# Expert feed-forward on one Trainium2 core: the gate's second pass moved behind its first, more work put in branches, a rare path moved to the start, an eighth weight buffer

## The chip, the cores and the metric

One Trainium2 chip, one of its cores. The time is device microseconds of one execution. Three runs of the kernel before took 1893.26, 1894.47 and 1895.01 us; the median is 1894.47. Fp32 weights lie in the chip's memory and are streamed once per execution.

## The reference, cut to what matters

256 tokens of width 1024 pass two layers (a pooling mixer with a dense feed-forward, then a delta-rule mixer with a mixture of experts) and a second block with three attentions and a feed-forward. The part around the change is the mixture of 8 experts, two for each token:

```python
def moe_ffn(h, router_w, router_b, w_gate, w_up, w_down):
    ...
    logits = (t @ router_w).astype(jnp.float32) + router_b.astype(jnp.float32)
    top_vals, top_idx = lax.top_k(logits, TOP_K)
    top_w = jax.nn.softmax(top_vals, axis=-1)
    gates = jnp.sum(jax.nn.one_hot(top_idx, N_EXPERTS, dtype=jnp.float32) * top_w[..., None], axis=1)
    for e in range(N_EXPERTS):
        y = swiglu(t, w_gate[e], w_up[e], w_down[e]).astype(jnp.float32)
        out = out + gates[:, e:e + 1] * y
```

Each expert has 1024 x 3584 gate and up weights and 3584 x 1024 down weights, 44 MB in all three. The kernel computes an expert only for the tokens that chose it, 64 on average.

## The kernel before, in words

**The weights.** `Stream.load` (L285 on) fetches one tile of the expert stream into the next buffer of the pool `rawm`, on SP's queue (L297). A tile holds 128 x 4096 floats (2 MB); the first two hold 128 x 2048. The pool has `RAWS_M` = 7 buffers. Tiles are loaded in the order of use (`plan_moe`): gate, up, then the down weights of the chunk before. A load goes out when its buffer's last readers are through.

**The experts.** `expert_loop` walks 8 experts x 4 chunks of the hidden width (1024, 1024, 1024, 512). A chunk of full width takes two tiles each of gate, up and down; the last chunk one each. `gather` (L1051) packs an expert's tokens into up to 128 columns by matmul. Per chunk, for the first 64 tokens ("main", L1108): gate, then SiLU on ACT (L1137), up, then the product `hid` on DVE (L1141), transposes (L1165), and the down matmuls (L1160) of the chunk before. For tokens 64 to 95 ("extra"): under `tc.If(count[e] > 64)` (L1142) both the gate's and the up's second passes stand together behind the up matmuls (L1114), into the PSUM tile `gx`; then `hidx` on ACT and DVE (L1146, L1147), its transposes (L1170) and their copy `hTx` (L1172), all in every chunk; and `extra_down` under a second `If` (L1175, matmuls L1122). The branches stand on PE only.

```python
with self.tc.If(count[e] > 64):
    extra(0, xg, wg, w // 4)
    extra(1, xg, wu, w // 4)
```

So gate, up and down tiles of a chunk are in use until the branch behind the up pass is through. The framework schedules the order on each engine itself and treats a branch's body as one unit; in the trace the branch stands ahead of the matmuls of the chunk's last up tile.

**The scatter.** When an expert's last down chunk is done, one chunk into the next expert, its rows are added to `h`: for each half of the tokens, matmuls with the first 64 rows (L1186), then with the second tokens' rows (L1189, always), then an add on DVE (L1193). The PSUM pool `most` has three buffers, called pt.

**The rare path.** `rare` (L1490 to L1498) covers experts with over 96 tokens. It issues loads ahead up to `RAWS_M - 2`, reads the largest count into a register of each engine (L1495) and branches twice (over 96, over 224; L1497). The body (`overflow`, L1500 on) holds all eight experts' work for 128 more tokens each, on PE, ACT, DVE and SP, with two weight buffers as its room. With these inputs it is never entered. It is called when expert 4 is done, one chunk into expert 5:

```python
if e0 == 4:
    self.rare(pg, pt, pd)
```

Of the kernel before, what the change touches and what calls it, by code (L numbers as in the profile page):

```python
# [9 lines left out]
F32 = mybir.dt.float32  # L10
# [10 lines left out]
KD = D // 128  # L21
# [4 lines left out]
FFC = (1024, 1024, 1024, 512)  # L26
RAW_D = 3072
RAW_M = 4096
RAWS_M = 7
FIRST_M = (2048, 2048)  # L30
SPARE_2 = list(range(2, 6)) + list(range(85, 91))
LN_EXP = "natural_log_exp_and_others"
# [291 lines left out]
class KB:  # L324
# [757 lines left out]
    def expert_loop(self, wk, pg, pt, pd):  # L1082

        nc, C, V = self.nc, self.C, self.nc.vector
        mm = nc.tensor.matmul
        st = self.stm
        self.pins[2] = 0
        lists, spreads = {0: self.gather(0, wk, pt)}, {}
        cnt = wk.tile([128, 1], F32, name="cntf", bufs=1)
        self.cnti = wk.tile([128, 1], I32, name="cnti", bufs=1)  # L1090
        counts = wk.tile([128, NE], I32, name="counts", bufs=1)
        V.tensor_copy(counts, self.pos[:, 2])
        V.tensor_reduce(cnt, self.pos[:, 2], axis=AX.X, op=OP.max)
        V.tensor_copy(self.cnti, cnt)
        gx = pg.tile([128, 2, 256], F32, name="gx")
        self.dx = pd.tile([128, 512], F32, name="dx")
        dx = self.dx[:, :256]
        for t in (gx, self.dx):
            V.memset(t, 0.0)
        chunks = [(e, c) for e in range(NE) for c in range(len(FFC))]  # L1100
        acc = {}
        count = {}
        prev = None

        def main(p, xg, ws, w):
            for k in range(KD):
                for s in range(2):
                    mm(p[s * 64:(s + 1) * 64, :w], xg[:, k, 0:64], ws[k][:, s * w:(s + 1) * w],  # L1108
                       start=k == 0, stop=k == KD - 1)

        def extra(r, xg, ws, w):
            for k in range(KD):
                for q in range(4):
                    mm(gx[q * 32:(q + 1) * 32, r, :w], xg[:, k, 64:96], ws[k][:, q * w:(q + 1) * w],  # L1114
                       start=k == 0, stop=k == KD - 1, skip_group_check=True)

        def extra_down(hTx, ws, c):
            n = len(ws) // 4
            for f, w in enumerate(ws):
                g, j = divmod(f, n)  # L1120
                for q in range(4):
                    mm(dx[q * 32:(q + 1) * 32], hTx[:, j, g * 32:(g + 1) * 32], w[:, q * 256:(q + 1) * 256],  # L1122
                       start=c == 0 and f == 0, stop=c == len(FFC) - 1 and f == len(ws) - 1, skip_group_check=True)

        for i in range(len(chunks) + 1):
            cur = None
            if i < len(chunks):
                e, c = chunks[i]
                w = FFC[c]
                if c == 0:  # L1130
                    count[e] = nc.values_load(counts[0:1, e:e + 1], engines=(mybir.EngineType.PE,), min_val=0, max_val=NT)
                xg = lists[e]
                wg = [st.plain("moe_w_gate") for _ in range(KD)]
                p = pg.tile([128, 512], F32, name="pg")
                main(p, xg, wg, w // 2)
                hid = wk.tile([128, 512], F32, name="hid")
                nc.scalar.activation(hid[:, :w // 2], p[:, :w // 2], AF.Silu)  # L1137
                wu = [st.plain("moe_w_up") for _ in range(KD)]
                p = pg.tile([128, 512], F32, name="pu")
                main(p, xg, wu, w // 2)  # L1140
                V.tensor_tensor(hid[:, :w // 2], p[:, :w // 2], hid[:, :w // 2], op=OP.mult)  # L1141
                with self.tc.If(count[e] > 64):  # L1142
                    extra(0, xg, wg, w // 4)
                    extra(1, xg, wu, w // 4)
                hidx = wk.tile([128, 256], F32, name="hidx")
                nc.scalar.activation(hidx[:, :w // 4], gx[:, 0, :w // 4], AF.Silu)  # L1146
                V.tensor_tensor(hidx[:, :w // 4], gx[:, 1, :w // 4], hidx[:, :w // 4], op=OP.mult)  # L1147
                if c == 1:
                    spreads[e] = self.spread(e, wk, pt)
                if c == 2 and e + 1 < NE:  # L1150
                    lists[e + 1] = self.gather(e + 1, wk, pt)
            if prev:
                e0, c0, hT, hTx = prev
                if c0 == 0:
                    acc[e0] = pd.tile([128, 512], F32, name="dacc")
                wd = [st.plain("moe_w_down") for _ in range(FFC[c0] // 128)]
                for f, wf in enumerate(wd):
                    s, j = divmod(f, len(wd) // 2)
                    for n in range(2):
                        mm(acc[e0][n * 64:(n + 1) * 64], hT[:, j, s * 64:(s + 1) * 64], wf[:, n * 512:(n + 1) * 512],  # L1160
                           start=c0 == 0 and f == 0, stop=c0 == len(FFC) - 1 and f == len(wd) - 1)
            if i < len(chunks):
                p = pt.tile([128, 4, 128], F32, name="pt")
                for j in range(w // 256):
                    nc.tensor.transpose(p[:, j], hid[:, j * 128:(j + 1) * 128], C["ident"])  # L1165
                cur_hT = wk.tile([128, 4, 128], F32, name="hT")
                nc.scalar.copy(cur_hT[:, :w // 256], p[:, :w // 256])  # L1167
                p = pt.tile([128, 2, 128], F32, name="pt")
                for j in range(w // 512):
                    nc.tensor.transpose(p[:, j], hidx[:, j * 128:(j + 1) * 128], C["ident"])  # L1170
                cur_hTx = wk.tile([128, 2, 128], F32, name="hTx")
                V.tensor_copy(cur_hTx[:, :w // 512], p[:, :w // 512])  # L1172
                cur = (e, c, cur_hT, cur_hTx)
            if prev:
                with self.tc.If(count[e0] > 64):  # L1175
                    extra_down(hTx, wd, c0)
            if prev and c0 == len(FFC) - 1:
                first, more = spreads.pop(e0)
                y = wk.tile([128, 512], F32, name="y", bufs=1)
                nc.scalar.copy(y, acc.pop(e0))  # L1180
                yx = wk.tile([128, 256], F32, name="yx", bufs=1)
                V.tensor_copy(yx, dx)
                for t in range(2):
                    ps = [pt.tile([128, 512], F32, name="pt") for _ in range(2)]
                    for n in range(2):
                        mm(ps[n], first[n * 64:(n + 1) * 64, t], y[n * 64:(n + 1) * 64], start=True, stop=True)  # L1186

                    for n in range(4):
                        mm(ps[n // 2][:, (n % 2) * 256:(n % 2 + 1) * 256], more[:, n, t], yx,  # L1189
                           start=False, stop=True, skip_group_check=True)  # L1190
                    for n in range(2):
                        hs = self.h[:, t, n * 512:(n + 1) * 512]
                        self.late = [V.tensor_tensor(hs, ps[n], hs, op=OP.add)]  # L1193
                if e0 == 4:
                    self.rare(pg, pt, pd)
            prev = cur

    def block2(self, st):
# [290 lines left out]

    def rare(self, pg, pt, pd):  # L1490

        t = self.stm.where[self.stm.i][0]
        while self.stm.next_load < min(t + RAWS_M - 2, len(self.stm.tiles)):
            self.stm.load()
        most = self.nc.values_load(self.cnti[0:1, 0:1], min_val=0, max_val=NT)  # L1495
        for first in (96, 224):
            with self.tc.If(most > first):  # L1497
                self.overflow(first, pg, pt, pd)  # L1498
# [81 lines left out]
def build(ctx, tc, I, out):  # L1580
# [6 lines left out]
    with kb.pool("mkv") as mkp:  # L1587
# [7 lines left out]
        with kb.pool("moe") as pl:  # L1595
# [4 lines left out]
            kb.wsps.close()  # L1600
            kb.stm.raw = raws.enter_context(kb.pool("rawm", RAWS_M, side="right"))
            kb.experts(raws)
# [24 lines left out]
```

## Time and profile before

| what | value |
|---|---|
| median of three runs | 1894.47 us |
| the profiled execution's own time | 1892.89 us |
| its span, first to last instruction | 1891.1 us |
| PE busy | 1758.4 us (93%) |
| DVE, ACT, POOL busy | 698.5, 594.6, 30.2 us |
| expert weights | 169 loads on SP's queue, 167 of 2048 KB |
| mean granted TensorE clock | 0.986 |

A busy share is a mean over stages: the expert stage lies between some 500 and 1413 us, and the rest of the span is the two dense parts around it. PE is TensorE's matmuls, PEld its weight loads, a q behind an engine's name its sequencer. In a timeline, a number in brackets behind a row is the engine's idle time before it and the arrow names what ended it.

### The profile page before, as it was taken

How to read it: one execution, taken by the hardware profiler on the slowest of the kernel's cores; microseconds unless marked ns; L12 is line 12 of the kernel's file. 1: busy time of each engine (PE TensorE's matmuls, PEld its weight loads, DVE VectorE, ACT ScalarE, POOL GpSimd, SP SyncE). 2: the span in 40 equal slices, each digit the busy share in tenths (PEclk: the TensorE clock that was granted, in tenths of full speed). 3: DMA queues.
4: the chain of work that ended last, by engine and by line, in shares of the span. 5: the costliest groups of instructions: out<-in, count | busy, mean ns of one | idle time of the engine just before them, and what ended most of it. 6: DMA issues, size and time to landing. Idle time of an engine off the chain costs nothing. (4 is left out here: it accounts for less than half of the span.)

```text
span 1891.1 us, 28195 instructions
## 1 busy us (share of the span) xinstructions
PE 1758.4 (93%) x12123; PEld 1201.5 (64%) x12123; DVE 698.5 (37%) x1365; ACT 594.6 (31%) x1043; POOL 30.2 (2%) x23
## 2 busy tenths in 40 slices
PE   7999999999887888889999889999987999999999
PEld 6898979998633333434434435344347778988987
DVE  6656578765400101000010100100016677665554
ACT  5544465445310101001010000100014657764443
POOL 0000000000000000000000000000002000002000
PEclk9999999999999999999999989999998999999999
DMA  8554543201499999999899989899943322445452
GB/s 328 198 192 179 179 169 122 101 35 56 189 425 425 426 425 426 425 425 384 360 377 425 379 361 383 338 425 426 374 199 134 134 101 101 179 156 201 179 189 79
DMA packets 40633, 501.55 MB, mean 265 GB/s; under 512 B 4497, under 2 KB 4881, under 8 KB 7441
## 3 DMA queue, kind: packets, MB, share of 16 engines
q1 hardware_dynamic: 40176, 498.59, 65.4%
q8 instruction: 129, 2.11, 0.5%
q10 hardware_dynamic: 288, 0.52, 0.1%
q14 instruction: 40, 0.32, 0.1%
HBM read 498.05 MB, written 1.05 MB: 264 GB/s over the span
## 5 line engine op out<-in xcount | busy, mean ns | idle before, releaser
L320 DVE TENSOR_TENSOR wlo<-raw,whi 128x1024 fp32r<-128x1024 f32 (+1 forms) x266 | 309.7, 1167 | 203.6 <-ACT whi L319 199.4
L319 ACT CAST whi<-raw 128x1024 fp32r<-128x1024 f32 (+1 forms) x276 | 274.0, 1000 | 262.9 <-PE pt L387 173.6
L386 PE MATMUL pt<-xTh,whi 128*128 128x256 f32 x1120 | 320.0, 286 | 3.8 <-ACT zT L786 1.5
L387 PE MATMUL pt<-xTl,whi 128*128 128x256 f32 x1120 | 318.6, 285 | 0.0
L388 PE MATMUL pt<-xTh,wlo 128*128 128x256 f32 x1120 | 318.0, 284 | 0.0
L1108 PE MATMUL pu<-raw,xg 128*64 128x512 f32 (+1 forms) x1024 | 208.6, 547 | 22.1 <-DMA raw<-in_w_moe_dram 16.3
L1108 PE MATMUL pg<-raw,xg 128*64 128x512 f32 (+1 forms) x1024 | 203.3, 546 | 21.1 <-DMA raw<-in_w_moe_dram 11.6
L386 PEld LDWEIGHTS pt<-xTh,whi 128*128 128x128 f32 x1120 | 212.5, 190 | 6.2 <-ACT zT L786 1.7
L387 PEld LDWEIGHTS pt<-xTl,whi 128*128 128x128 f32 x1120 | 212.3, 190 | 1.4 <-DVE xTl L393 0.3
L388 PEld LDWEIGHTS pt<-xTh,wlo 128*128 128x128 f32 x1120 | 211.8, 189 | 0.8 <-issue 0.5
L1160 PE MATMUL dacc<-raw,hT 128*64 128x512 f32 x896 | 204.4, 598 | 7.1 <-DMA raw<-in_w_moe_dram 4.7
L1147 DVE TENSOR_TENSOR hidx<-gx,hidx 128x256 f32<-128x256 f32 (+1 forms) x32 | 12.5, 391 | 494.0 <-ACT hidx L1146 494.0
L1108 PEld LDWEIGHTS pu<-raw,xg 128*64 128x64 f32 x1024 | 77.9, 138 | 141.4 <-issue 119.1
L1108 PEld LDWEIGHTS pg<-raw,xg 128*64 128x64 f32 x1024 | 79.0, 138 | 138.8 <-issue 114.9
L1137 ACT ACTIVATE hid<-pg 128x512 f32<-128x512 f32 (+1 forms) x32 | 17.4, 544 | 400.2 <-PE pg L1108 400.1
L1160 PEld LDWEIGHTS dacc<-raw,hT 128*64 128x64 f32 x896 | 62.5, 136 | 119.9 <-issue 109.4
L386 PE MATMUL acc<-whi,hidh 128*128 128x512 f32 x216 | 84.9, 395 | 0.9 <-ACT whi L319 0.9
L387 PE MATMUL acc<-wlo,hidh 128*128 128x512 f32 x216 | 85.4, 395 | 0.3 <-DVE wlo L320 0.3
L388 PE MATMUL acc<-whi,hidl 128*128 128x512 f32 x216 | 85.4, 395 | 0.0
L1114 PE MATMUL gx<-raw,xg 128*32 128x256 f32 (+1 forms) x1536 | 75.1, 353 | 0.0
L1167 ACT COPY hT<-pt 128x512 f32<-128x512 f32 (+1 forms) x32 | 17.0, 532 | 170.3 <-PE pt L1165 170.3
L1141 DVE TENSOR_TENSOR hid<-pu,hid 128x512 f32<-128x512 f32 (+1 forms) x32 | 20.0, 625 | 133.7 <-PE pu L1108 133.7
(438 smaller groups left out, 2112.7 us busy)
## 6 DMA issues: line engine op xcount, KB each, us to landing
raw<-in_w_moe_dram SPq DMA_DIRECT2D x167, 2048.0 KB, 20.4
raw<-in_w_second_dram SPq DMA_DIRECT2D x44, 1536.0 KB, 6.4
raw<-in_w_first_dram SPq DMA_DIRECT2D x39, 1536.0 KB, 6.5
grow<-in_rows_dram SPq DMA_DIRECT2D x9, 512.0 KB, 4.3
raw<-in_w_moe_dram SPq DMA_DIRECT2D x2, 1024.0 KB, 6.7
raw<-in_w_first_dram SPq DMA_DIRECT2D x3, 512.0 KB, 7.2
cst<-in_cst_dram SPq DMA_DIRECT2D x1, 1124.0 KB, 16.1
raw<-in_w_first_dram SPq DMA_DIRECT2D x1, 1088.0 KB, 5.5
```

The costliest lines, as they stand in the source:

```text
L319: nc.scalar.copy(hi[:, :n], raw)
L320: eng.tensor_tensor(lo[:, :n], raw, hi[:, :n].bitcast(F32), op=OP.subtract)
L386: mm(out, l[0], r[0], start=first, stop=False)
L387: mm(out, l[0], r[1], start=False, stop=False)
L388: mm(out, l[1], r[0], start=False, stop=last)
L1108: mm(p[s * 64:(s + 1) * 64, :w], xg[:, k, 0:64], ws[k][:, s * w:(s + 1) * w], start=k == 0, stop=k == KD - 1)
L1114: mm(gx[q * 32:(q + 1) * 32, r, :w], xg[:, k, 64:96], ws[k][:, q * w:(q + 1) * w], start=k == 0, stop=k == KD - 1, skip_group_check=True)
L1137: nc.scalar.activation(hid[:, :w // 2], p[:, :w // 2], AF.Silu)
L1141: V.tensor_tensor(hid[:, :w // 2], p[:, :w // 2], hid[:, :w // 2], op=OP.mult)
L1147: V.tensor_tensor(hidx[:, :w // 4], gx[:, 1, :w // 4], hidx[:, :w // 4], op=OP.mult)
L1160: mm(acc[e0][n * 64:(n + 1) * 64], hT[:, j, s * 64:(s + 1) * 64], wf[:, n * 512:(n + 1) * 512], start=c0 == 0 and f == 0, stop=c0 == len(F ...
L1167: nc.scalar.copy(cur_hT[:, :w // 256], p[:, :w // 256])
```

## The change

It sets the number of weight buffers to 8 and shrinks the scratch for descriptors to 1024. It calls `rare` at the start of `expert_loop`, behind the first gather, with the six first loads issued ahead. It gives the gate's extra pass a branch of its own directly behind the gate's main pass, and the up's one behind the up pass. The transposes of `hidx` and the second tokens' scatter matmuls come under branches too; the transposes now write to the first half of `gx` (`tx`) and not to a pt buffer.

```diff
-RAWS_M = 7
+RAWS_M = 8
...
-        dx = self.dx[:, :256]
+        dx, tx = self.dx[:, :256], gx[:, 0].rearrange("p (j f) -> p j f", j=2)
         for t in (gx, self.dx):
             V.memset(t, 0.0)
+        self.rare(pg, pt, pd)
...
-        def extra(r, xg, ws, w):
-            for k in range(KD):
-                for q in range(4):
-                    mm(gx[q * 32:(q + 1) * 32, r, :w], xg[:, k, 64:96], ws[k][:, q * w:(q + 1) * w],
-                       start=k == 0, stop=k == KD - 1, skip_group_check=True)
+        def extra(e, r, xg, ws, w):
+            with self.tc.If(count[e] > 64):
+                for k in range(KD):
+                    for q in range(4):
+                        mm(gx[q * 32:(q + 1) * 32, r, :w], xg[:, k, 64:96], ws[k][:, q * w:(q + 1) * w],
+                           start=k == 0, stop=k == KD - 1, skip_group_check=True)
...
                 main(p, xg, wg, w // 2)
+                extra(e, 0, xg, wg, w // 4)
...
-                with self.tc.If(count[e] > 64):
-                    extra(0, xg, wg, w // 4)
-                    extra(1, xg, wu, w // 4)
+                extra(e, 1, xg, wu, w // 4)
...
-                p = pt.tile([128, 2, 128], F32, name="pt")
-                for j in range(w // 512):
-                    nc.tensor.transpose(p[:, j], hidx[:, j * 128:(j + 1) * 128], C["ident"])
+                with self.tc.If(count[e] > 64):
+                    for j in range(w // 512):
+                        nc.tensor.transpose(tx[:, j], hidx[:, j * 128:(j + 1) * 128], C["ident"])
                 cur_hTx = wk.tile([128, 2, 128], F32, name="hTx")
-                V.tensor_copy(cur_hTx[:, :w // 512], p[:, :w // 512])
+                V.tensor_copy(cur_hTx[:, :w // 512], tx[:, :w // 512])
...
-                    for n in range(4):
-                        mm(ps[n // 2][:, (n % 2) * 256:(n % 2 + 1) * 256], more[:, n, t], yx,
-                           start=False, stop=True, skip_group_check=True)
+                    with self.tc.If(count[e0] > 64):
+                        for n in range(4):
+                            mm(ps[n // 2][:, (n % 2) * 256:(n % 2 + 1) * 256], more[:, n, t], yx,
+                               start=False, stop=True, skip_group_check=True)
...
-                if e0 == 4:
-                    self.rare(pg, pt, pd)
...
     def rare(self, pg, pt, pd):
 
-        t = self.stm.where[self.stm.i][0]
-        while self.stm.next_load < min(t + RAWS_M - 2, len(self.stm.tiles)):
+        while self.stm.next_load < RAWS_M - 2:
             self.stm.load()
...
-    nc = _bacc.Bacc("TRN2", target_bir_lowering=False, num_devices=1)
+    nc = _bacc.Bacc("TRN2", target_bir_lowering=False, num_devices=1, dynamic_dma_scratch_size=1024)
```

## Rows read from the trace of the kernel before

**Rows 1.** Windows: length, busy us of PE, PEld, DVE, ACT, POOL; PEclk; DMA share, GB/s.
```profile
498.00:816.77 318.77, 270.09 (x1384) 117.98 (x1385) 37.85 (x108) 33.92 (x72) 0.00 (x0) 0.98 1.01 424
816.77:946.77 130.00, 123.76 (x1154) 57.07 (x1155) 10.07 (x21) 9.31 (x20) 0.00 (x0) 1.00 0.92 387
946.77:1041.55 94.78, 89.98 (x483) 38.88 (x481) 10.16 (x21) 9.20 (x20) 0.00 (x0) 1.00 0.96 401
1041.55:1181.65 140.10, 127.85 (x1156) 59.27 (x1153) 9.38 (x19) 9.33 (x20) 0.00 (x0) 0.96 0.91 373
```

**Rows 2.** The view of the tile gx: PE's matmuls, ns min/median/max, first and last start.
```profile
L1114 PE MATMUL gx<-raw,xg x1536: 272/379/403, 830.2 to 1385.1; 128*32 128x256 f32 x144, 128*32 128x128 f32 x48
```

**Rows 3.** PE's timeline: start, us, what, [idle before it], from 820 on.
```profile
821.58 3.65 PE L1108 MATMUL pg<-raw,xg 128*64 128x512 f32 x16 [1.15 <-DMA raw<-in_w_moe_dram]
826.58 3.65 PE L1108 MATMUL pu<-raw,xg 128*64 128x512 f32 x16 [1.35 <-DMA raw<-in_w_moe_dram]
...
1049.37 3.65 PE L1108 MATMUL pu<-raw,xg 128*64 128x512 f32 x16 [0.75 <-DMA raw<-in_w_moe_dram]
...
1284.11 3.65 PE L1108 MATMUL pu<-raw,xg 128*64 128x512 f32 x16 [0.60 <-DMA raw<-in_w_moe_dram]
```

**Rows 4.** PE's timeline behind the rare path.
```profile
1092.15 8.75 PE L1108 MATMUL pg<-raw,xg 128*64 128x512 f32 x26 [9.27 <-DVEq L1497]
```

**Rows 5.** The view of line 1497, the rare path's branches: ns min/median/max, starts.
```profile
L1497 SPq EVENT_SEMAPHORE  x16: 17/17/17, 1065.5 to 1087.8; - x16
...
L1497 SPq COMPARE_BRANCH  x2: 45/48/50, 1059.8 to 1084.8; - x2
L1497 PEldq COMPARE_BRANCH  x2: 3577/4318/5059, 1082.1 to 1085.9; - x2
```

**Rows 6.** The view of the expert weights, one load in each window: start and landing.
```profile
L297 SPq DMA_DIRECT2D raw<-in_w_moe_dram x1: 451/451/451, 500.9 to 500.9; - x1
...
DMA to landing us min/median/max: 26.7/26.7/26.7
...
L297 SPq DMA_DIRECT2D raw<-in_w_moe_dram x1: 425/425/425, 1058.8 to 1058.8; - x1
...
DMA to landing us min/median/max: 25.9/25.9/25.9
...
L297 SPq DMA_DIRECT2D raw<-in_w_moe_dram x1: 346/346/346, 1092.2 to 1092.2; - x1
...
DMA to landing us min/median/max: 8.9/8.9/8.9
```

**Rows 7.** The timeline at expert 4's scatter, PE and DVE.
```profile
1070.86 1.99 PE L1189 MATMUL pt<-yx,og 128*128 128x256 f32 x8
1072.03 0.69 DVE L1193 TENSOR_TENSOR h<-pt,h 128x512 f32<-128x512 f32 x1 [5.91 <-PE pt L1189]
...
1072.78 1.13 PE L1186 MATMUL pt<-y,og 64*128 64x512 f32 x4
```

**Rows 8.** The view of line 1142, a branch that is skipped; PE's timeline in expert 4.
```profile
L1142 PEldq COMPARE_BRANCH  x44: 65/185/1760, 521.2 to 1384.5; - x44
...
986.23 3.65 PE L1108 MATMUL pu<-raw,xg 128*64 128x512 f32 x16 [0.16 <-PEq L1142]
...
991.16 0.38 PE L1170 MATMUL pt<-cst,hidx 128*128 128x128 f32 x2
991.38 1.50 PE L1051 MATMUL pt<-oh,hn 128*128 128x128 f32 x12
```

**Rows 9.** PE's timeline in expert 3: extra matmuls of a branch that is entered.
```profile
864.16 7.11 PE L1114 MATMUL gx<-raw,xg 128*32 128x256 f32 x128
```

**Rows 10.** Timelines of PE and DVE: transposes of hid, and the product hidx.
```profile
990.67 0.66 PE L1165 MATMUL pt<-cst,hid 128*128 128x128 f32 x4 [0.78 <-DVE hid L1141]
...
1083.36 0.43 DVE L1147 TENSOR_TENSOR hidx<-gx,hidx 128x256 f32<-128x256 f32 x1 [6.80 <-ACT hidx L1146]
```

**Rows 11.** PE's timeline in expert 0's last chunk, behind a skip.
```profile
594.26 5.36 PE L1108 MATMUL pu<-raw,xg 128*64 128x256 f32 x31 [2.38 <-issue]
```

## The prediction, made before the change was run

> **What bounds the kernel now.** The page first: PE is busy for most of the span, but slices 11 to 30, the expert stage, are also those in which the weight stream runs at its highest rate. A share over the span can't tell which of the two ends last, so I cut the stage at each expert's first gate matmul and read the windows [rows 1]. Experts 0 to 2: 318.77 us, DMA share 1.01, PE busy 270.09. There the stream is the bound and PE has 48 us to spare. Expert 3 takes 130.00 us, expert 4 94.78, expert 5 140.10, at DMA shares of 0.92, 0.96 and 0.91. From expert 3 on it is PE, and DMA idles. (Expert 6 took 94.79 and expert 7 to its last scatter 136.49; they repeat 4 and 3.) What makes experts heavy are the extra matmuls: 1536 of them [rows 2], 128 a chunk of full width, hence 12 chunks, hence three experts: 3, 5 and 7. The others skip.
>
> Next, which waits PE has left after expert 3 began at 816.77. On DMA only four: 1.15 and 1.35 in expert 3's first chunk, and 0.75 and 0.60 at the first up tile of experts 5 and 7 [rows 3]. So from 830 to the end of the stage each microsecond taken from PE is one gained, as long as tiles arrive; before 816 a microsecond counts only if the stream gets or loses it. This is the frame for all that follows.
>
> **Part 1: the path for over 96 tokens leaves expert 5.** It is skipped here (no expert has over 96), and skipping costs PE an idle of 9.27 us [rows 4]. Expert 5 against expert 3, DMA waits taken out: 140.10 - 0.75 - (130.00 - 2.50) = 11.9 us; the granted clock of expert 5 (0.96 against 1.00, rows 1) is why this is more than the idle. Ends: 9.3 (the idle alone) and 11.9. I take **-11.9**, the comparison of whole experts.
>
> **Part 2: what it costs at its new place.** PE: its two compare-and-branch instructions took 3.58 and 5.06 us, one behind the other [rows 5]. They now stand between the gather and the first gate matmul, which moves back by some 10. Cover: the 48 us that PE has to spare in experts 0 to 2. If that were gone, 10 us would come back. POOL and ACT have nothing there that PE doesn't already wait for.
>
> SP is another matter. SP too goes through both branches, and behind each it has eight semaphore instructions [rows 5]. Those of the first ran from 1065.5 on and the second compare stood at 1084.8; the last weight load issued before (1058.8) landed 25.9 us later, at 1084.7 [rows 6]. So I read it as: SP's skip waits until every load in flight has landed. SP then finished at 1087.8, and the stream was dry. At the new place six loads are issued ahead of it (RAWS_M - 2). The sixth load of before was issued at 500.9 and landed 26.7 us later, at 527.6 [rows 6]. The second skip took SP 1084.8 to 1087.8 = 3.0 us; with 0.5 around it (an estimate) the next load is issued at 531.1. The first load into a dry queue landed 8.9 us after issue [rows 6]: 540.0, where the seventh load would have come 4.95 us behind the sixth (2.097 MB at the 424 GB/s of [rows 1]), at 532.5. That is 7.5 later for the first; the shortest reading (3.0 + 8.9 - 4.95 with nothing between) gives 7.0. Everything up to expert 3 hangs on the stream, so its start moves by as much. Ends: 0 (if SP's order differs and nothing drains) and 11 (held on to 1092.2 as here, 4 us more, where load and PE both came behind DVE [rows 4, 6]; at the new place DVE is through before SP, so I don't expect that). I take **+7.0**, the shortest reading.
>
> **Part 3: second tokens' scatter branched.** Eight matmuls fill 1070.86 to 1072.78, twice per expert: 3.85 us [rows 7]. Experts 2, 4 and 6 (light) scatter inside experts 3, 5 and 7, where PE is the bound; those of 0 and 1 are covered by the stream. Against it: two skips, and the second half's second pt buffer must wait for the add of the first (three pt buffers, four needed), which the removed matmuls hid. An add takes 0.69 [rows 7]; some 0.5 shows, an estimate. 3.85 - 0.35 - 0.5 = 3.0, ends 2.2 and 3.85. Three times: **-9.0**.
>
> **Part 4: the gate's extra pass in a branch of its own, transposes in another.** A skip shows on PE as 0.16 us of idle; the median compare-and-branch takes 0.185, the longest 1.76 [rows 8]. Two transposes fill 991.16 to 991.38, 0.22 [rows 8]. Per light expert: about -0.95 for transposes, 8 added skips +1.6, net +0.65; experts 4 and 6 count: **+1.3**, ends -1.9 (skips free) and +2.9. In heavy experts a branch that is entered shows nothing: the extra matmuls of 864.16 follow without an idle mark [rows 9]. One gain: in expert 3's first chunk the gate's half of the 7.11 us of extras needs no up tile and fills the 1.35 of [rows 3]: **-1.35**, ends 0 and that. In the chunks after it no wait on DMA is left to fill.
>
> [...] The trace shows 0.16 us for a near skip and 3.58 to 5.06 us for the far ones. [...] The skips of today jump over 128 matmuls with their weight loads [rows 2] and show 0.16, so the sum goes by 0.17.
>
> **Part 5: eighth buffer and gate tiles freed earlier.** No PE time. It is the cover for Parts 1 and 3. A chunk holds six tiles (two gate, two up, two down), so seven buffers are one ahead; the waits of 0.75 and 0.60 are what that leaves behind a light expert. A light expert of about 91 us needs 21 tiles of 4.95 = 104 us, so it eats 13 us of lead, against 9 now. One more buffer is 4.95, gate tiles given back before the up pass more. I expect both waits gone: **-1.35**, ends 0 and that. The smaller descriptor scratch costs nothing: the page lists DMA issues from SP and ACT alone, none from POOL.
>
> **Sum.** -11.9 + 7.0 - 9.0 + 1.3 - 1.35 - 1.35 = **-15.3 us**. The profiled span is 1891.1, its own time 1892.89: it becomes 1875.8 and 1877.6. The median of the three runs, 1894.47, lies 1.6 above that execution: 1879.2, forecast **1879**. All ends on the good side give -28, all on the bad side about -2.
>
> **The rivals.**
> (a) *SP's skip drains nothing, or the 0.8 us wait goes.* Without the +7.0: 1872. Or: each chunk pays 0.78 us waiting for hid [rows 10]; if the up pass's extras now stand behind the up matmuls, they hide it in 12 chunks, -9.4: 1870. Against: the scheduler put the extras ahead of the last up tile before, and may again. 0.15 together.
> (b) *The transposes wait for hidx.* They need ACT's and DVE's work on the last extras; that product began at 1083.36 and took 0.43, ending 0.9 after the extras (1082.88 by rows 4) [rows 10]. If PE stands at its branch for that in each heavy chunk: 12 x 0.9 = 10.8, so 1890. Today other matmuls lie between. 0.13, with it the case that supply still fails behind experts 4 and 6 and eats some 6 of Part 3 (1885).
> (c) *Skips that miss.* This one ends slower. There was a PE idle of 2.38 us that nothing released, in the chunk whose up pass follows a skip [rows 11], and a compare of 1.76 [rows 8]. The PE-bound part gets 22 more skips (16 in experts 4 and 6, 6 at scatters). At 1.76 each instead of 0.17: +35, 1914. It turns slower from 1.05 us a skip. Against: experts 4 and 6 came out at 94.78 and 94.79, each with eight skips. Chance 0.10. [...]
> (d) *The change doesn't do what it says:* extras stay behind the up pass whatever the code says. Then buffers free later, Part 5 rests on the eighth alone; within the forecast's range.
>
> **How the numbers follow.** The forecast with its own range (1875 to 1885) 0.62, (a) 0.15, (b) 0.13, (c) 0.10. The range 1868 to 1890 takes in (a) and (b) and leaves out (c) and the far ends. Within 0.2% (3.8 us, about what a measurement of this kernel can tell from no change) falls a part of (b): 0.06. Slower by more: 0.09. Faster: 0.85.
>
> **What would show it.** Right: windows of expert 5 at about 127 us and of 4 and 6 near 91; no idle at line 1497 behind 530; a dry stream of some 7 us near 525 to 533; expert 3's first gate matmul near 824. Wrong: an expert 3 start at 817 (no drain) or beyond 830; light experts above 96 with idles at branches (c); idles before the second tokens' transposes in heavy chunks (b); waits on DMA after expert 3 (Part 5).

## The result, and the profile after

Slower, where faster was forecast: the changed kernel took 1905.49 us (median of 1903.39 to 1906.32), the kernel before beside it 1893.87. The ratio is 1.006, with a 95% interval of 1.0042 to 1.0077. The forecast was 1879, its range 1868 to 1890. The profiled execution took 1906.04 with a span of 1904.2, so the span grew by 13.1.

The windows of the changed kernel, cut within 0.1 us of each expert's first gate matmul, with the columns of [rows 1]; experts 0 to 2 in the first, then 3 to 7:

```profile
534.11:827.64 293.53, 262.09 (x1256) 106.00 (x1258) 25.96 (x56) 26.72 (x58) 0.00 (x0) 0.99 1.00 423
827.64:957.94 130.30, 125.60 (x1139) 54.74 (x1141) 9.97 (x21) 9.34 (x20) 0.00 (x0) 1.00 0.99 415
957.94:1057.64 99.70, 93.48 (x477) 39.04 (x475) 10.15 (x21) 9.23 (x20) 0.00 (x0) 1.00 0.97 404
1057.64:1187.64 130.00, 125.58 (x1141) 54.70 (x1139) 9.36 (x19) 9.34 (x20) 0.00 (x0) 1.00 0.94 370
1187.64:1287.44 99.80, 93.49 (x476) 39.04 (x474) 9.55 (x19) 9.23 (x20) 0.00 (x0) 1.00 0.97 403
1287.44:1425.90 138.46, 133.44 (x1179) 56.31 (x1175) 12.19 (x22) 9.54 (x22) 1.30 (x2) 1.00 0.73 293
```

Three things are to be seen. Expert 3 starts at 827.56, 10.8 later than before. Expert 5 is 10.1 shorter, less than the rare path alone should give, though it lost scatter matmuls too; the prediction wanted 127. And the light experts 4 and 6, which lost matmuls and gained only skips, went from 94.8 to 99.7. Of those 4.9 us, 3.5 are busy time (93.48 against 89.98), not idle.

**Where in the light experts.** PE's groups over experts 3 to 7, first of the kernel before, then of the changed one (columns: instruction, count | busy us, mean ns | idle before, releasers). The first line of each is the up pass:

```profile
L1108 PE MATMUL pu<-raw,xg 128*64 128x512 f32 (+1 forms) x640 | 129.2, 543 | 4.2 <-DMA raw<-in_w_moe_dram 2.7 <-PEq L1142 1.2
```

```profile
L1109 PE MATMUL pu<-raw,xg 128*64 128x512 f32 (+1 forms) x640 | 146.1, 543 | 2.7 <-PEq L1113 0.6
L1166 PE MATMUL pt<-cst,hid 128*128 128x128 f32 x70 | 11.9, 287 | 14.7 <-DVE hid L1144 14.7
```

The same 640 rows, of the same mean length, cover 16.9 us more, and the idle in front of them has shrunk. Rows that lie over each other count once in the busy time (640 of 543 ns add up to 347.5 us), so what changed is their overlap. PE's timeline of the changed kernel shows where, first in expert 4 (light), then in expert 5 (heavy):

```profile
961.64 3.65 PE L1109 MATMUL pg<-raw,xg 128*64 128x512 f32 x16 [0.16 <-PEq L1113]
965.09 4.82 PE L1109 MATMUL pu<-raw,xg 128*64 128x512 f32 x18
970.07 3.62 PE L1109 MATMUL pu<-raw,xg 128*64 128x512 f32 x14
974.47 0.66 PE L1166 MATMUL pt<-cst,hid 128*128 128x128 f32 x4 [0.78 <-DVE hid L1144]
...
1075.38 1.07 PE L1109 MATMUL pu<-raw,xg 128*64 128x512 f32 x2
1076.50 0.41 PE L1171 MATMUL gx<-cst,hidx 128*128 128x128 f32 x2
1076.84 3.65 PE L1109 MATMUL pu<-raw,xg 128*64 128x512 f32 x14
1081.28 0.66 PE L1166 MATMUL pt<-cst,hid 128*128 128x128 f32 x4 [0.79 <-DVE hid L1144]
```

The code puts the transposes of `hidx` behind those of `hid`; the scheduler put their branch into the up pass's last tile, behind two of its 16 rows. A matmul of the program shows as two rows here (16 in the code for a chunk's up pass, 32 in the trace), and two matmuls, whose results go to partitions 0 to 63 and 64 to 127, run side by side (the first four rows of the x14 start at 1076.84, 1076.85, 1077.32 and 1077.33): a whole tile of 16 starts its successor 3.45 us later (961.64 to 965.09), 0.43 for each two rows. The x2, one matmul without its partner, takes 1.07. Of the seven matmuls in the x14 one runs alone as well, the last: its two rows start at 1079.47 and 1079.90 with nothing beside them. In the light chunk, where the branch is skipped, the cut stands between x18 and x14 with no idle marked at all: 965.09 to 974.47 is 9.38, where the uncut pass of run 2 below takes 8.21.

**At the start.** The view of line 1496 of the changed kernel, the rare path's two branches, answers to [rows 5]; behind it the first gate matmul, and the seventh load of weights with its landing, as in [rows 6]:

```profile
L1496 SPq EVENT_SEMAPHORE  x16: 17/17/17, 519.3 to 533.9; - x16
L1496 SPq COMPARE_BRANCH  x2: 45/48/50, 510.8 to 529.8; - x2
L1496 PEldq COMPARE_BRANCH  x2: 4897/5878/6858, 521.7 to 528.8; - x2
...
  PEq L1496: 19.2, 1
...
L297 SPq DMA_DIRECT2D raw<-in_w_moe_dram x1: 346/346/346, 534.4 to 534.4; - x1
...
DMA to landing us min/median/max: 8.9/8.9/8.9
```

SP was at its second compare at 529.8, half a microsecond after the sixth load had landed (529.3), and issued the seventh at 534.4, which landed at 543.3. With a running stream it would have come 4.9 behind the sixth (as in run 5: 528.28 and 533.18), at 534.2: 9.1 us of dry stream. PE's first gate matmul moved from 512.36 to 534.11, by 21.8 and not by some 10; expert 3's start shows only what the stream lost (run 5).

**The scatter** behind a light expert, answering to [rows 7], is as wanted: from 1086.56 to the next gate matmul at 1089.87, the removed matmuls gone and the adds hidden.

```profile
1086.56 1.13 PE L1187 MATMUL pt<-y,og 64*128 64x512 f32 x4 [0.67 <-ACT y L1181]
1087.87 1.85 PE L1187 MATMUL pt<-y,og 64*128 64x512 f32 x4 [0.18 <-PEq L1189]
1089.87 3.65 PE L1109 MATMUL pg<-raw,xg 128*64 128x512 f32 x16
```

Of the four DMA waits of [rows 3] none is left. The one that remains is 1.35 in front of expert 3's first matmul, still in expert 2's window; the kernel before has the same one, ahead of those of [rows 3]. First before, then changed:

```profile
816.77 3.65 PE L1108 MATMUL pg<-raw,xg 128*64 128x512 f32 x16 [1.35 <-DMA raw<-in_w_moe_dram]
```

```profile
827.56 3.65 PE L1109 MATMUL pg<-raw,xg 128*64 128x512 f32 x16 [1.35 <-DMA raw<-in_w_moe_dram]
```

### The profile page after: what moved, and what is told of

Its sections match the earlier page's. It is cut to its first block, busy times and chain, and to the rows that moved or that the text cites. A ratio compares the mean times of both kernels' runs of the same rounds, so it can differ in the third digit from the quotient of the medians.

```text
span 1904.2 us, 28201 instructions
## 1 busy us (share of the span) xinstructions
PE 1772.8 (93%) x12008; PEld 1193.9 (63%) x12008; DVE 697.6 (37%) x1365; ACT 595.1 (31%) x1043; POOL 30.2 (2%) x23
## 3 DMA queue, kind: packets, MB, share of 16 engines
HBM read 498.05 MB, written 1.05 MB: 262 GB/s over the span
## 5 line engine op out<-in xcount | busy, mean ns | idle before, releaser
L1109 PE MATMUL pu<-raw,xg 128*64 128x512 f32 (+1 forms) x1024 | 232.8, 543 | 10.9 <-DMA raw<-in_w_moe_dram 5.9
L1109 PE MATMUL pg<-raw,xg 128*64 128x512 f32 (+1 forms) x1024 | 208.5, 546 | 30.1 <-PEq L1496 19.2
L1109 PEld LDWEIGHTS pu<-raw,xg 128*64 128x64 f32 x1024 | 84.0, 137 | 141.9 <-issue 125.1
L1116 PEld LDWEIGHTS gx<-raw,xg 128*32 128x32 f32 x1536 | 45.7, 110 | 37.9 <-issue 16.3
```

## The experiments

Each is the changed kernel with one edit, or a run before it with one more. The kernel before, timed again beside each set, had medians of 1892.77 to 1893.13 (1893.87 beside the changed kernel), so the times compare across sets within about a microsecond.

**1. Transposes outside a branch.**

```diff
-                with self.tc.If(count[e] > 64):
-                    for j in range(w // 512):
-                        nc.tensor.transpose(tx[:, j], hidx[...], C["ident"])
+                p = pt.tile([128, 2, 128], F32, name="pt")
+                for j in range(w // 512):
+                    nc.tensor.transpose(p[:, j], hidx[...], C["ident"])
```

> The changed kernel, but the transposes of hidx stand outside a branch and write to a pt buffer, as in the kernel before; all else as changed. Theory: the transposes' branch splits the up pass between the two column halves of one step and drains PE. In the trace of the changed kernel two matmuls and the gap behind them take 1.17 us where two take 0.43 (0.74 a chunk in light experts, some 0.8 in heavy ones beyond the transposes themselves). From expert 3 on that is 20 chunks, 15.5 us, less 1.9 for the light experts' transposes that come back: about 13.5 faster than the changed kernel, 1892 us (0.999 of before), experts 4 and 6 at 97.7, experts 3 and 7 some 3 shorter. Rival (the loss lies in the gate's own branch and in the start alone): within 3 us of 1905.

Measured 1884.22, ratio to before 0.9951 (0.9937 to 0.9964): 21.3 us less than the changed kernel, where 13.5 was expected. From expert 3's first matmul to the last scatter it is 578.3 against 598.4. PE's groups of this kernel, and the same place of expert 5 in its timeline:

```profile
L1109 PE MATMUL pu<-raw,xg 128*64 128x512 f32 (+1 forms) x640 | 127.9, 542 | 2.0 <-PEq L1113 1.2 <-issue 0.5
L1171 PE MATMUL pt<-cst,hidx 128*128 128x128 f32 x35 | 7.1, 272 | 0.0
...
1067.20 3.65 PE L1109 MATMUL pu<-raw,xg 128*64 128x512 f32 x16
1071.65 0.66 PE L1166 MATMUL pt<-cst,hid 128*128 128x128 f32 x4 [0.80 <-DVE hid L1144]
1072.14 0.38 PE L1171 MATMUL pt<-cst,hidx 128*128 128x128 f32 x2
```

The up pass is back at 127.9, 18.2 of the 20. From the last up tile to the transposes of `hid` it takes 4.45, where the cut tile took 5.90 (1075.38 to 1081.28). The transposes' branch costs 20 us in all; 21 if one counts that run 1's expert 4 takes 97.3 and its expert 6 96.3, with an idle of 0.51 in expert 4's last chunk that nothing released.

**2. The branch kept, but held behind the transposes of hid.** Is it the branch or its place?

```diff
-                    nc.tensor.transpose(p[:, j], hid[...], C["ident"])
+                    last = nc.tensor.transpose(p[:, j], hid[...], C["ident"])
...
-                with self.tc.If(count[e] > 64):
+                with self.tc.issue_after(last.ins), self.tc.If(count[e] > 64):
```

> The changed kernel, with the branch of the second block's transposes kept, but held behind the transposes of hid, so that it no longer splits a pair of matmuls of the up pass. Theory (the place of the branch is the cost: the split pair and the wait inside the up pass): all but a skip of 0.35 in each light chunk goes, so 1884 to 1888, beside 1884.2 with no branch at all. Rival (the branch itself is the cost, wherever it stands): 1900 to 1905.

Measured 1885.11, 0.9961 (0.9947 to 0.9976). The up pass of expert 4 in this kernel is whole again, and the skip stands behind the transposes:

```profile
960.15 7.43 PE L1109 MATMUL pu<-raw,xg 128*64 128x512 f32 x32
968.36 0.66 PE L1166 MATMUL pt<-cst,hid 128*128 128x128 f32 x4 [0.78 <-DVE hid L1144]
969.34 1.94 PE L1124 MATMUL dx<-raw,hTx 128*32 128x256 f32 x32 [0.32 <-PEq L1169]
```

So it is the place. The branch alone is worth nothing: from the transposes of `hid` to the next matmuls it is 0.98 with the skip (968.36 to 969.34), and 0.81 with the two transposes run always (1190.26 to 1191.07 in run 1). Nor is it the transposes' new place in `gx`, which run 2 keeps.

In heavy chunks the transposes (128\*128 in the rows) stand among matmuls of 128\*64. But light chunks skip them and lose nearly as much (0.93 net per full chunk against 1.2 to 1.5), so the transposes themselves are not the bulk of it. In heavy chunks no run here separates their share, or that of their wait for `hidx`, from the cut's.

**3. What one more skip costs.** Run 1 with the gate's second pass in two branches of half the matmuls.

```diff
-            with self.tc.If(count[e] > 64):
-                for k in range(KD):
+            for ks in (range(KD),) if r else (range(KD // 2), range(KD // 2, KD)):
+                with self.tc.If(count[e] > 64):
+                    for k in ks:
```

> Transposes outside a branch (1884.2), and the second pass of the gate in two branches of half the matmuls each, so one branch more in every chunk. Theory (a near skip costs 0.35 from the start of the last matmul before it to the first behind, and an entered branch between matmuls next to nothing): light chunks behind expert 3 longer by 0.3 to 0.4 each (27.90 becomes 28.25), heavy ones by under 0.2; time 1886 to 1889. Rival (0.17, the idle that the profile marks): light chunks longer by 0.17, time 1885.5. [...]

Measured 1892.27, 0.9995 (0.9985 to 1.0005): 8 more than run 1, where 2 to 5 was expected; of its profiled execution, the shortest of ten (1889.99 against run 1's 1883.58), it is 6.4. The size of one skip came out: the second chunk of each light expert went from 27.90 to 28.25. Heavy chunks paid more than the 0.2 allowed, 0.45 and 0.24 in an expert's first two. The rows of run 1 show it as well, a gate tile with a skip behind it and one without:

```profile
1174.82 3.60 PE L1109 MATMUL pg<-raw,xg 128*64 128x512 f32 x16
1178.59 3.65 PE L1109 MATMUL pg<-raw,xg 128*64 128x512 f32 x16 [0.16 <-PEq L1113]
1182.04 3.63 PE L1109 MATMUL pu<-raw,xg 128*64 128x512 f32 x16
```

3.77 against 3.45: the skip costs 0.32 from start to start, and the mark shows half of it, because a tile of 16 lasts 3.65 and its successor otherwise starts before its end. Another part of the miss is again a place. In this kernel the scheduler moved a skip of the scatter between the two halves of a pair, in the first chunk of experts 4 and 6 (29.69 against 28.42); here in expert 6:

```profile
1202.77 1.12 PE L1188 MATMUL pt<-y,og 64*128 64x512 f32 x2
1204.04 1.09 PE L1188 MATMUL pt<-y,og 64*128 64x512 f32 x2
```

**4. Both extra passes under one branch again, behind the up pass.** The transposes' branch stays.

```diff
-                extra(e, 0, xg, wg, w // 4)
...
-                extra(e, 1, xg, wu, w // 4)
+                with self.tc.If(count[e] > 64):
+                    extra(0, xg, wg, w // 4)
+                    extra(1, xg, wu, w // 4)
```

> The changed kernel with both extra passes under one branch behind the up pass, as before; the transposes' branch, the scatter's branch, the moved path and 8 buffers stay. Theory: each skip costs PE 0.35 us from start to start (not the 0.16 of the idle mark), an entered branch some 0.2: 8 and 12 of them less from expert 3 on, 2.8 + 2.4 = 5 us: 1900. No wait on DMA after expert 3 in spite of the later release, since the eighth buffer covers it. Rival (the gate tiles' early release carries the gain): waits on DMA return in experts 5 and 7, about 1.4 us, and the time is 1902 or more.

A miss: 1910.37, 1.0089 (1.0075 to 1.0102). Two DMA waits are back in expert 3's first chunk (1.05 and 1.35); at experts 5 and 7 there is none. Light experts did get shorter where expected (their third chunk from 25.03 to 24.16), but the last, half-width chunks of experts 4 and 6 grew from 16.53 to 19.92 and 22.42, 9.3 together. The view of the branch's line in this kernel, and the timeline at those two places:

```profile
L1143 PEldq COMPARE_BRANCH  x44: 65/179/6617, 516.3 to 1402.9; - x44
...
1046.13 1.72 PE L1109 MATMUL pu<-raw,xg 128*64 128x256 f32 x6 [1.96 <-PEq L1143]
...
1278.97 1.94 PE L1109 MATMUL pu<-raw,xg 128*64 128x256 f32 x6 [3.23 <-PEq L1143]
```

Compares of 3.93 and 5.24 us stand at these two places (1041.8 and 1273.4), where the median is 0.18; the longest, 6.62, stands at 547.9 in expert 0, where the stream is the bound. So what rival (c) feared happens here, and not in the changed kernel, whose longest near compare takes 1.1:

```profile
L1113 PEldq COMPARE_BRANCH  x88: 65/180/1097, 512.9 to 1396.8; - x88
```

The body is twice as long here, but its length doesn't decide it: the kernel before has the same long body and at most 1.76 [rows 8], and behind the short bodies single compares took 2.96 us in run 1 (1028.7) and 4.84 in run 2 (553.4, with PE standing for 2.27, in expert 0). So whether two shorter branches are safer than one isn't shown; why one compare of 44 takes 6.6 and most 0.18 no run here shows either.

**5. The rare path back behind expert 4.**

```diff
-        self.rare(pg, pt, pd)
...
+                if e0 == 4:
+                    self.rare(pg, pt, pd)
...
-        while self.stm.next_load < RAWS_M - 2:
+        t = self.stm.where[self.stm.i][0]
+        while self.stm.next_load < min(t + RAWS_M - 2, len(self.stm.tiles)):
```

> The changed kernel with the path for over 96 tokens back behind expert 4. Theory: at the start it costs the stream 9.1 us (the seventh load lands at 543.3, not 534.2), which comes out one to one; behind expert 4 it costs PE 11.9. So 2.8 us slower than the changed kernel: 1908, expert 3 starting near 818, expert 5 at 142. Rival 1 (the start is free, covered by PE's spare time): 11.9 slower, 1917, expert 3 still starts near 827. Rival 2 (the start costs what PE lost there, 20 us): 8 faster, 1897.

A hit: 1908.26, 1.0078 (1.0064 to 1.0092). Expert 3 starts at 817.5, expert 5 takes 141.7. The move brings 11.7 and costs 10.0, of which 1.1 is a first load that goes out later (499.0 against 497.9).

**6. The scatter of second tokens without a branch.**

```diff
-                    with self.tc.If(count[e0] > 64):
-                        for n in range(4):
-                            mm(ps[n // 2][...], more[:, n, t], yx, ...)
+                    for n in range(4):
+                        mm(ps[n // 2][...], more[:, n, t], yx, ...)
```

> The changed kernel with the second tokens' scatter matmuls outside a branch. Theory: in the trace of the changed kernel the light scatters take 3.3 us and took 5.96 before: 2.65 x 3 = 8 us slower, 1913.5. Rival (the scatter's branch gives nothing, since the add on DVE sets the pace): within 2 us of 1905.

Measured 1916.73, 1.0126 (1.0111 to 1.0142): 11.2 more, not 8. One scatter takes 5.96 (1089.00 to the gate at 1094.96) against the 3.31 above, so 2.65 each and 8 in all. From expert 3's first matmul to the last scatter the profile has 12.7 more (611.1 against 598.4), with expert 3 starting 2.0 earlier. The rest is a place once more: the gate's branch now cuts a gate tile behind its sixth row, and the second chunk of all five experts grows by 0.7 to 1.0, in the light ones from 28.84 to 29.82.

```profile
1089.00 1.13 PE L1187 MATMUL pt<-y,og 64*128 64x512 f32 x4 [0.68 <-ACT y L1181]
...
1094.96 1.93 PE L1109 MATMUL pg<-raw,xg 128*64 128x512 f32 x6
...
1223.05 1.93 PE L1109 MATMUL pg<-raw,xg 128*64 128x512 f32 x6
1225.13 6.19 PE L1109 MATMUL pg<-raw,xg 128*64 128x512 f32 x26 [0.15 <-PEq L1113]
```

**7 to 10. The rare path's drain.** All four stand on run 1. First, one branch for both passes in place of two, at the start:

```diff
-        for first in (96, 224):
-            with self.tc.If(most > first):
-                self.overflow(first, pg, pt, pd)
+        with self.tc.If(most > 96):
+            room = [self.stm.raw.tile([128, RAW_M], F32, name="raw") for _ in range(2)]
+            for first in (96, 224):
+                self.overflow(first, pg, pt, pd, room)
```

> Transposes outside a branch (1884.2), and the path for over 96 tokens at its new place under one branch for both passes in place of two. Theory (the second compare on SP, 3.65 us, stands between the landing of the sixth load and the issue of the seventh): the seventh load lands 3.7 to 4.5 earlier, near 538, expert 3 starts as much earlier, near 823, and the time is 1880. Rival (the drain lasts until the sixth landing plus something that a longer jump makes up): 1884, no change.

Measured 1879.88, 0.9937 (0.992 to 0.9953), the seventh load at 538.2, expert 3 at 823.2. Then the same branch behind expert 4:

> The same single branch, put back behind expert 4, where the path stood before. Theory (at the start only the stream pays, behind expert 4 TensorE does): expert 3 starts near 817 (9 earlier than at the start with two branches), expert 5 is longer by what one far branch leaves, some 7 of the 11.9 (that of before had two), so 1884.2 - 9.1 + 7 = 1882; between 1879 and 1887. Rival (the jump's length is the cost, one branch costs what two did): expert 5 longer by 11.9, 1887.

Measured 1880.79, 0.9936 (0.992 to 0.9953): expert 3 at 818.7, expert 5 6.5 longer than expert 3. With one branch either place costs about the same. Then the single branch ahead of the gather, and the path's own loads moved to POOL's queue:

```diff
+        self.gate()
+        self.rare(pg, pt, pd)
+        lists[0] = self.gather(0, wk, pt)
...
-            nc.sync.dma_start(r[:, :w], ...)
+            nc.gpsimd.dma_start(r[:, :w], ...)
```

> As the single branch at the start, but the path's own loads are issued from GpSimd's queue (so that SP's skip has no loads of its own to settle) and the path stands ahead of the gather. Theory (SP's skip waits for every load in flight because the body issues loads on SP's semaphores): the seventh load is issued before the sixth has landed, lands near 533, expert 3 starts near 818, time 1875. Rival (a skip on SP waits for loads in flight whatever the body holds): the stream is dry as before, 1880.

Measured 1874.47, 0.9908 (0.9891 to 0.9924). SP no longer has the semaphore instructions behind its branch; they stand on POOL, and the seventh load goes out at 520.2, eight microseconds before the sixth lands (528.2), and lands at 533.1. The views of the branch's line and of that load in this kernel:

```profile
L1494 POOLq EVENT_SEMAPHORE  x4: 17/43/43, 513.8 to 514.0; - x4
...
L297 SPq DMA_DIRECT2D raw<-in_w_moe_dram x1: 337/337/337, 520.2 to 520.2; - x1
```

And as its counterpart, ahead of the gather with the loads back on SP's queue:

> As the run with the path ahead of the gather and its loads on GpSimd's queue (1874.5), but the path's loads back on SP's queue. Theory (it is the loads in the body that make SP's skip wait for those in flight): the seventh load lands near 538 and expert 3 starts near 823, as with one branch behind the gather, 1879 to 1880. Rival (being ahead of the gather was what helped): 1874 to 1875.

Measured 1879.41, 0.9927 (0.991 to 0.9943). SP's semaphore instructions are back, and the last one stands where the sixth load has landed (528.2):

```profile
L1494 SPq EVENT_SEMAPHORE  x8: 17/17/17, 517.1 to 528.5; - x8
```

So being ahead of the gather brings nothing. What drains the stream here is that the skipped body has loads of its own on SP's queue: with them there, SP's skip lasts until the loads in flight have landed (its last semaphore instruction at 528.5, the landing at 528.2), without them it doesn't (the seventh load out at 520.2).

**11. Seven buffers,** with run 1 (`RAWS_M = 7`).

> Transposes outside a branch (1884.2), seven buffers in place of eight. Theory (the eighth is cover for the light experts): waits on DMA of 0.5 to 5 come back at the starts of experts 5 and 7 and in expert 3's first chunk, 1886 to 1892. Rival (gate tiles freed earlier suffice): no such wait, 1884.

The rival held: 1884.16, 0.9955 (0.9939 to 0.9972); no DMA wait but the 1.35 at expert 3's start that run 1 has too. The eighth buffer is worth nothing here. What took away the waits at experts 5 and 7 is not settled: they are gone with the gate's tiles freed earlier and seven buffers (here), and gone with the late release and eight (run 4), and in both kernels light experts take longer than the 94.8 of before, which gives the stream time.

**12. A better version.** The waits for `hid` in front of its transposes, 14.7 us over experts 3 to 7 in the changed kernel, have other work of PE right behind them. On the run with POOL's queue, the transposes are held behind the first tile of the down pass:

```diff
+                    if i < len(chunks) and f == len(wd) // 2 - 1:
+                        with self.tc.issue_after(ins.ins):
+                            cur = turn()
```

(`turn` holds the transposes of `hid` and `hidx` and their copies, unchanged.)

> As the run with the path ahead of the gather and its loads on GpSimd's queue (1874.5), with the transposes of hid and hidx held behind the first tile of the down pass, so that the wait for hid before them (0.79 in three chunks of an expert, 0.53 in the fourth) has work in its place. Theory (the order of TensorE's own instructions is what this stage hangs on): 2.9 per expert from expert 3 on, five experts, so 14.5 less and 1860; heavy experts 125.4 become 122.5, light ones 96.3 become 93.4. Rival (the stream or the copies behind the transposes take the place of the wait): waits on DMA or ACT in experts 4 to 7, over 1868.

Measured 1858.17, ratio to before 0.9813 (0.9796 to 0.9829): 16.3 less than the run it stands on, 14.5 expected. Its windows of experts 3 and 4, and the group of the transposes, now without idle:

```profile
818.60:940.80 122.20, 120.87 (x1137) 53.97 (x1139) 9.87 (x21) 9.33 (x20) 0.00 (x0) 1.00 1.01 425
940.80:1033.90 93.10, 90.44 (x483) 40.72 (x481) 10.16 (x21) 9.22 (x20) 0.00 (x0) 1.00 1.00 423
...
L1155 PE MATMUL pt<-cst,hid 128*128 128x128 f32 x70 | 12.0, 289 | 0.0
```

The stream runs at 1.00 there too, and PE has no wait on DMA after expert 3's first matmul, so the two are about even up to expert 6.

## Why the prediction was wrong

The frame held: stream up to expert 3, PE behind it. Step by step, in microseconds of the span, forecast against measured:

| step | forecast | measured | from |
|---|---|---|---|
| Part 1, expert 5 without the rare path | -11.9 | -11.7 | run 5 |
| Part 2, stream dry at the start | +7.0 | +9.1 | landing of the seventh load |
| Part 3, scatter branched, three times | -9.0 | -8.0 | run 6 |
| Part 4, branches at gate and transposes | +1.3 | +25.8 | 21.1 by run 1 (20.1, and 1.0 that run 1's own expert 4 lost), 4.65 below |
| Part 4, gate's half fills a wait | -1.35 | -2.5 | both waits of [rows 3] in expert 3's first chunk gone; back in run 4 |
| Part 5, waits at experts 5 and 7 | -1.35 | -1.35 | gone; through which of its causes is open (run 11) |
| first load later (499.0 against 497.3) | | +1.7 | not of the change: 497.4 to 499.2 in the other runs |
| sum | -15.3 | +13.1 | span: +13.1 |

**The step that failed is Part 4,** which put the new branches at +1.3 where they cost 25.8, at three places.

First and largest, "about -0.95 for transposes" took the transposes' branch as a skip in each chunk of experts 4 and 6, at the place where the code has it. The scheduler moved it into the up pass's last tile, where it cuts a pair of matmuls that run side by side. That costs 0.93 net in a full light chunk, 1.2 to 1.5 in a full heavy one and 0.6 to 0.7 in one of half width: 21 in all. Runs 1 and 2 show it. Rival (b) had a transposes' branch that makes heavy chunks wait, at 0.9 each, but held it unlikely for "Today other matmuls lie between." They lay between because the transposes were not a unit then; made one, it stands in the up pass, and the weight load for them did wait for `hidx`, 8.1 us in nine chunks, with 0.7 of idle on PE. That a skip could cost by where it stands, in light chunks too, was in no rival.

Second, "a skip shows on PE as 0.16 us of idle" took a mark for a price. From start to start it is 0.32 to 0.35 (run 3); the sum had 0.2 (eight for 1.6).

Third, "a branch that is entered shows nothing" is true of the idle column, not of the time. Run 1's heavy expert takes 125.4, where 130.00 less its DMA waits (2.50) and the scatter (2.65) is 124.85: 0.55 is left for the four chunks' added branch. Its light expert takes 96.3 against 94.79: 1.5. So 3 x 0.55 + 2 x 1.5 = 4.65.

**Part 2** named the mechanism and mis-sized it: the "3.0" from the second compare to the end took 4.2 (529.75 to 533.92), and 0.4 before it and 0.5 behind it, which the shortest reading put at nothing, make 9.1. That PE would move back by some 10 was short by half (21.8), but it stayed covered. Runs 7, 9 and 10 show the mechanism itself.

**Part 3** was right within 1 us, and its two skips and the add came out at 1.2 of the 3.85. **Rival (c)** had the right side for another reason: no near compare of the changed kernel takes more than 1.1, though some of run 4 do. As a sign of it the prediction wanted "idles at branches"; the light experts did pass 96, yet 3.5 of their 4.9 stood in the busy time. Its "turns slower from 1.05" is 0.87 by its own terms (15.3 / 22 + 0.17). The second half of **rival (a)** didn't occur: the waits for `hid` are 14.7 here and 13.1 before.

## What to carry to other kernels

Ask of every branch you add where the scheduler will put it, and read the engine's order there: here a skip between whole tiles costs 0.3 us and one within a pair of matmuls that run side by side 1.2, and neither the idle column nor the mean duration shows it, only the busy time of a group whose count hasn't changed, or the distance from start to start. In this program a skipped body that issues loads on the streaming queue drains that queue; put its loads on another queue (5 us, run 9 against 10), and put both passes under one branch (4 us, run 7). Removing 0.2 us of always-run work by a branch isn't worth a branch.

## What was not expected of the hardware

Two rows of one engine's timeline can lie over each other so that a cut loses time with no idle marked: 640 rows of the up pass, of mean 542 and 543 ns, cover 127.9 us uncut (run 1) and 146.1 cut once in each of 20 chunks.

A skip is not of one price. Near compares took 0.065 to 1.1 us in the changed kernel, up to 1.76 in the kernel before, up to 4.8 in run 2 and up to 6.6 in run 4, on the same data. After the long compare before 1046.13 in run 4, in which PE stood for 1.96, the granted clock of the next 4 us was 0.57, against 1.00 in the 4 us before it:

```profile
1042.00:1046.00 4.00, 2.17 (x21) 1.38 (x16) 0.00 (x0) 0.47 (x2) 0.00 (x0) 1.00 1.02 426
1046.00:1050.00 4.00, 3.71 (x18) 2.00 (x20) 0.58 (x2) 0.19 (x1) 0.00 (x0) 0.57 1.00 422
```
